# Weight sums of the attention stage on GpSimd, moved tiles of stage two, and one hand-written order for stages 3 to 5

## The chip, the cores and the metric

The kernel runs on one core of a Trainium2 chip. Its engines work side by side, each through its own queue in order: TensorE (PE; its weight loads are shown apart as PEld), VectorE (DVE), ScalarE (ACT), GpSimd (POOL) and SyncE (SP), which here only issues DMAs. GpSimd issues DMAs too, among its other work. An instruction starts when everything ahead of it in its queue has gone and the semaphores that it waits for have been raised. The metric is the device time of one launch in microseconds (us), the median of several runs.

## The reference, cut to what matters

One layer of a streaming encoder over 2048 prompt tokens and 64 sample tokens, width 1024. Three sub-layers follow each other, each with a norm ahead and one behind, whose result is added to the residual:

```python
y = token_mixer(rms_norm(x, g_mixpre), ...)         # gated convolution + matrix memory, one output projection
x = x + rms_norm(y, g_mixpost)
y = memory_attend(rms_norm(x, g_mempre), mk, mv, w_q, w_o)   # 4 heads, 256 memory tokens
x = x + rms_norm(y, g_mempost)
up = causal_dwconv(rms_norm(x, g_ffnpre) @ w_up, ff_buf, w)  # 2 x 2816 columns, width 3
a, g = jnp.split(up, 2, axis=-1)
x = x + rms_norm((gelu(g) * a) @ w_down, g_ffnpost)
```

All matrices are float32. The kernel keeps the precision by splitting an operand into a high part and a remainder and adding three products (high x high, high x remainder, remainder x high).

## The kernel before

The program has five stages, written by `phase1` to `phase5`. Stage 1 projects the input, stage 2 runs the matrix memory and the output projection and leaves x1 in memory, stage 3 is the attention and leaves x2, stage 4 is the up-projection with the convolution, and stage 5 is the down-projection. PE works nearly throughout.

**Splits.** `split` (lines 102 and 103) makes the high part on ScalarE and the remainder on VectorE, or on GpSimd where it is asked for. `mm3` (lines 116 to 118) issues the three products. One split tile is thus written by two engines before PE may read it.

**Stage 2 and the place of A.** The tiles come from pools that are stacked on the left side of SBUF: ld, wp, wk and l2, in that order. When stage 2 ends, stage 3 lays A (64 KB in each partition) and behind it B on the same place. A holds the keys multiplied into the query projection, B the values multiplied into the output projection. A tile of stage 3 waits for the last reader of whatever lay in its place. In wp lie, in this order, the two yn tiles, from which x1 is stored, the gain gb, the residual xt, the second half of the output weights and the states cn.

**Start of stage 3.** PE makes 32 blocks pA of A, six PSUM tiles deep. Each is evicted into A by ScalarE (line 108) and VectorE (line 109). In this part ScalarE, VectorE and GpSimd keep the written order. One tile of raw values, raw4, is loaded three times and is split on GpSimd twice.

**Loop of stage 3.** 16 groups of 128 tokens. A round of PE is: scores (sc, two halves of 24 products), transposition of x of a later group (line 1073, tile tp), a half of the output product (yo), transposition of the finished rows of the group before (line 1229, `x2_T`), then the rest of yo with a transposition of the softmax between. Lines 1073 and 1229 take turns on three PSUM tiles tp, so that the second half of line 1229 needs a tp that VectorE has emptied (the remainder xs, line 103). `x2n` needs a reciprocal root that GpSimd computes by a power (line 96, r2), `post` one more (por), `score` a third (rsr).

**Weight sums.** Beside this, `sums` prepares stage 4, which computes its products by a scheme with seven instead of eight block products and needs sums of weight blocks. 44 pieces of 512 KB are loaded by SP in four DMAs each into a buffer of three, four sums of 128x256 are formed (lines 1141 to 1144), and GpSimd stores the piece. From the fourth round on there are four pieces in a round until they run out. SP also loads the rows xr of x1 for each round, which wait until line 1229 has read the rows before.

**What sets the order.** Within `manual_schedule` the named engines keep the order in which the code is written; the other engines are ordered by a scheduler. PE is in such an order in stages 2 to 5, SP in the loop of stage 3 and in stage 4. In stage 5 SP is ordered by the scheduler, and in its last part ScalarE, VectorE and GpSimd keep the written order.

**Stage 5.** `need` loads and splits a group of 256 tokens of the activations (hr into hh), `load_down` loads and splits the three or four weight tiles of a part (raw into dh and dl).

Of the kernel before, what the change touches and what calls it, by code (L numbers as in the profile page):

```python
# [14 lines left out]
P = 128  # L15
D = 1024
# [16 lines left out]
GROUPS = [(0, 392), (392, 384), (776, 384), (1160, 384)]  # L33
NB = 352
NPASS = T // (2 * NB)
PARTS = [3, 3, 4, 4, 4, 4]
CG = dict(mix=0, mem=8, kv=16, ffn=24, mnw=32, cw=36, fw=48)
CST_W = 48 + 132
# [28 lines left out]
class Prog:  # L67
# [68 lines left out]
    def build(self):  # L136
        tc, nc = self.tc, self.nc
        with ExitStack() as es:
            cp = self.pool(es, "const")

            self.pool(es, "edge", side="right").pool.tile([P, 8], F32, name="edge")
            self.rawp = self.pool(es, "raw", side="right")
            self.ident = cp.tile([P, P], F32, name="ident")
            make_identity(nc, self.ident)
            self.ones = cp.tile([P, P], F32, name="ones")
            nc.vector.memset(self.ones, 1.0)
            sm = cp.tile([P, 16 + 2 * NT], F32, name="small")
            self.mhalf, self.bg = sm[:, 0:8], sm[:, 8:16]
            self.r_all, self.rk_all = sm[:, 16:16 + NT], sm[:, 16 + NT:]
            nc.vector.memset(self.mhalf, -0.5)  # L150
            self.cst = cp.tile([P, CST_W], F32, name="cst")
            self.dma(self.cst, self.a["cst"])
            self.dma(self.bg, self.a["bg"].partition_broadcast(P))
            self.G = cp.tile([P, NT, 8], F32, name="G")
            self.aT = cp.tile([P, NR], F32, name="aT")
            self.em = cp.tile([P, NR], F32, name="em")
            self.wsb = cp.tile([P, NR], F32, name="wsb")
            self.wcb = cp.tile([P, NR], F32, name="wcb")
            dt = tc.dram_tile
            self.yaT = dt([4, P, T], F32, name="yaT")  # L160
            self.x2T = dt([KT, P, T], F32, name="x2Td")
            self.hd = dt([NF, P, T], F32, name="hd")
            self.wsd = dt([NF, P, 4, D // 2], F32, name="wsd")
            self.qT = dt([4, P, T], F32, name="qTd")
            self.kvo = dt([T, KVO], F32, name="kvo")
            self.nmd = dt([NR, P], F32, name="nmd")
            self.wd = dt([NR, P], F32, name="wd")
            self.mkd = dt([KT, P, NM], F32, name="mkd")
            self.mvd = dt([KT, P, NM], F32, name="mvd")
            self.od = dt([P, KT, NS_TOK], F32, name="od")  # L170
            self.ys = dt([NS_TOK, D], F32, name="ysd")
            self.x1 = dt([T, D], F32, name="x1d")
            self.x2 = dt([T, D], F32, name="x2d")
            self.pe = mybir.EngineType.PE
            self.zes = es.enter_context(ExitStack())
            self.qes = es.enter_context(ExitStack())
            self.fl_es = ExitStack()
            self.fl = self.pool(self.fl_es, "fill", space=PSUM)
            self.phase1()
            self.phase2()  # L180
            self.phase3()
            self.phase4()
            self.phase5()


    def phase1(self):
# [541 lines left out]
    def phase2(self):  # L728
        tc, nc, a = self.tc, self.nc, self.a
        V = nc.vector  # L730
        with ExitStack() as es:
# [9 lines left out]
            py_ = self.pool(es, "p2py", bufs=3, space=PSUM)  # L741
            ld.tile([P, 16], F32, name="padl")
            wk.tile([P, 16], F32, name="padw")
            yns = [wp.tile([P, D], F32, name="yn2%d" % i) for i in range(2)]
            gb = wp.tile([P, D], F32, name="gb2")
            xt_ = wp.tile([P, D], F32, name="xt2")
            wo1 = wp.tile([P, 2, 4, D], F32R, name="wo1")
            wo = lambda part, k, sl: (self.wo0(part, k) if k < 4 else wo1[:, part, k - 4])[:, sl]
            cn = {16: wp.tile([P, H, VW], F32, name="cn_s"), 0: wp.tile([P, H, VW], F32, name="cn_p")}

            def load_wo(k):
                raw = self.raw(a["w_out"][k])
# [225 lines left out]
    def phase3(self):  # L978
# [6 lines left out]
        A = lambda part, k, sl: ap[:, part, k, sl]  # L985
        B = lambda part, k, sl: bp[:, part, k, sl]
        with ExitStack() as es:
            es.enter_context(tc.manual_schedule(engines={self.pe}))
            py_ = self.pool(es, "p3py", bufs=3, space=PSUM)
            with ExitStack() as es0:  # L990
                zw = self.wop.tile([P, 7168], F32R, tag="w", name="zw")
                raw4 = self.wop.tile([P, D], F32, tag="w7", name="raw4")
                mv = zw[:, 0:4096].rearrange("p (a k m) -> p a k m", a=2, k=KT)
# [59 lines left out]
            self.em_es.close()  # L1053
            self.wo_es.close()

            es.enter_context(tc.manual_schedule(engines={mybir.EngineType.SP}))
            zq = self.zq = self.pool(self.qes, "zq", side="right")
            zq.tile([P, 32], F32, name="padq")
            wx = self.pool(es, "p3x", side="right")
# [70 lines left out]
            def sums():  # L1130

                KH = KT // 2
                for f in range(NF):
                    for q in range(2):
# [3 lines left out]
                            for h in range(2):  # L1138
                                self.dma(t[:, i + 2 * h], src[:, h].rearrange("p k c -> p (k c)"))
                        a11, a21, a12, a22 = (t[:, i] for i in range(4))  # L1140
                        V.tensor_tensor(out=a22, in0=a21, in1=a22, op=ALU.add)
                        V.tensor_tensor(out=a21, in0=a11, in1=a21, op=ALU.subtract)
                        V.tensor_tensor(out=a11, in0=a22, in1=a11, op=ALU.subtract)
                        V.tensor_tensor(out=a12, in0=a12, in1=a11, op=ALU.subtract)
                        self.store(self.wsd[f, :, :, q * 2 * P:(q + 1) * 2 * P], t)
                        yield

# [87 lines left out]
    def phase4(self):  # L1235
# [12 lines left out]
        self.zes.close()  # L1248
        self.zes = ExitStack()
        with ExitStack() as es:  # L1250
            es.enter_context(tc.manual_schedule(engines={self.pe, mybir.EngineType.SP}))
            left = self.pool(es, "p4l")
            early = self.pool(es, "p4e", side="right")
            right = self.pool(es, "p4r", side="right")
# [45 lines left out]
            def w_split(w, n):  # L1300
                if w is None:
                    return
                if n == "wd":
                    o = left.tile([P, 2, KH, P], F32R, tag="wd", name="wd", bufs=1)
                else:
                    o = first.pop(n, None)
                    if o is None:
                        o = w_op(n, 2 if n == "wc" else 1)
                self.split(o[:, 0], o[:, 1], w.r[n])
                w.o[n] = o  # L1310
# [100 lines left out]

            tk = t_load(0)
            w = w_load(0, ("wb",), tk.w)
            w_split(w, "wa")
            t_split(0, tk, "B11", tk.r["R11"])
            t_split(0, tk, "B21", tk.r["R21"])
            v = head1(0, w, tk.o)
            t_adds(tk)
            t_split(0, tk, "T2", tk.X)
            w_split(w, "wb")  # L1420
            head2(v, tk.o)
            t_split(0, tk, "T1", tk.r["R12"])
# [76 lines left out]
    def phase5(self):  # L1499
        tc, nc, a = self.tc, self.nc, self.a  # L1500
        V = nc.vector
        with ExitStack() as es:
            es.enter_context(tc.manual_schedule(engines={self.pe}))
            ac0 = self.pool(es, "p5a")
            w0 = self.pool(es, "p5w")
            ac1 = self.pool(es, "p5b")
# [36 lines left out]
            def need(i):  # L1543
                if i < len(work) and i not in hs:
                    pi, t0 = work[i]
                    hs[i] = load_h(f0s[pi], PARTS[pi], t0)
            ws = {0: load_down(0, 0, PARTS[0])}
            need(0)
            held = None
            tail = None  # L1550
            for i, (pi, t0) in enumerate(work):
                last = pi == len(PARTS) - 1
                if t0 == groups[3] and pi + 1 < len(PARTS):
                    ws[pi + 1] = load_down(pi + 1, f0s[pi + 1], PARTS[pi + 1])
                if i == len(PARTS):
                    self.dma(gpost, a["g_ffnpost"].partition_broadcast(P))
                if last and tail is None:
# [1 line left out]
                                                                        mybir.EngineType.DVE, mybir.EngineType.Pool})) or 1  # L1559
                need(i)  # L1560
                need(i + 1)
                h = hs.pop(i)
                for j in range(t0 // P, (t0 + min(2 * P, T - t0) + P - 1) // P):
                    w = tw(j)
# [116 lines left out]
```

## Time and profile before

| | us |
|---|---|
| median of 3 runs | 2924.99 |
| lowest and highest | 2923.73, 2928.92 |
| the profiled execution | 2930.46 |
| its span, first to last instruction | 2928.8 |
| PE busy | 2839.5 (97%) |
| DVE, ACT, POOL busy | 1718.0, 1205.7, 383.4 |

Times in the rows further below count from the start of the span. A row of the timeline says when an instruction or a run of equal ones began, how long it took, and in brackets how long the engine had stood idle before it and who released it. By the matmuls' starts stage 2 ends at about 1008 us, the loop of stage 3 lies between 1071 and 1492 us, stage 4 begins with a matmul at 1501 us, and stage 5 with one at 2414 us.

### The profile page before, as it was taken

What the parts mean: (1) busy time and instruction counts of PE and PEld (TensorE: products, weight loads), DVE (VectorE), ACT (ScalarE), POOL (GpSimd) and SP (SyncE); (2) the same over time, 40 slices, a digit from 0 to 9 for tenths busy, and PEclk for the clock granted to TensorE, in tenths of its full rate; (3) what the DMA queues carried; (4) which work ended last, traced back from release to release, by engine and by line L of the source; (5) the groups of instructions that cost most, each with busy time, mean ns of one, the idle gap of its engine ahead of it and who ended that gap; (6) DMA issues with size and microseconds to landing.
All of it is one profiled execution on the core that took longest, in us unless ns stands there. A gap on an engine that the chain in (4) does not pass through costs nothing.

```text
span 2928.8 us, 41744 instructions
## 1 busy us (share of the span) xinstructions
PE 2839.5 (97%) x15906; PEld 2625.9 (90%) x15906; DVE 1718.0 (59%) x2815; ACT 1205.7 (41%) x2463; POOL 383.4 (13%) x608
## 2 busy tenths in 40 slices
PE   8999999999999999999979999999999999999998
PEld 8999999998888877778769999999999988888887
DVE  6413422355666565566567778877887772534459
ACT  5224223233444353332345656566666654101113
POOL 1111011112212111222100000000000000000026
PEclk9999999999999999999989999999999999999999
DMA  8434332147676344677456454654454543322126
GB/s 279 149 100 126 106 114 91 60 150 268 217 223 220 101 145 135 219 235 252 158 183 216 153 174 136 218 173 153 151 181 156 175 132 102 96 62 81 58 79 214
DMA packets 211498, 456.84 MB, mean 156 GB/s; under 512 B 25414, under 2 KB 113672, under 8 KB 211298
## 3 DMA queue, kind: packets, MB, share of 16 engines
q1 hardware_dynamic: 180418, 346.14, 37.6%
q0 software_dynamic: 28720, 100.17, 9.0%
q10 hardware_dynamic: 2160, 7.87, 0.9%
q8 instruction: 125, 2.05, 0.3%
q14 instruction: 75, 0.61, 0.1%
HBM read 345.56 MB, written 108.54 MB: 155 GB/s over the span
## 4 chain that ended last, share of the span: by engine, by line
PE 51%; DVE 6%; DMA 3%; issue 2%; SPq 1%; ACT 1%; POOL 0%; DVEq 0%; POOLq 0%; ACTq 0%
PE up L116 10%; PE up L118 10%; PE up L117 10%; PE y L117 4%; PE y L118 4%; PE y L116 4%; DMA sums<-in_w_up 3%; DVE acc L568 1%; SPq L72 1%; PE yo L116 1%; PE yo L117 1%; PE yo L118 1%; PE sc L116 1%; PE sc L118 1%; PE sc L117 1%
## 5 line engine op out<-in xcount | busy, mean ns | idle before, releaser
L116 PE MATMUL y<-dh,hh 128*128 128x512 f32 x704 | 275.0, 391 | 5.1 <-ACT dh L102 5.1
L117 PE MATMUL y<-dl,hh 128*128 128x512 f32 x704 | 274.8, 390 | 2.4 <-DVE dl L103 2.4
L118 PE MATMUL y<-dh,hh 128*128 128x512 f32 x704 | 274.8, 390 | 0.0
L116 PE MATMUL mm<-xs,wh 128*128 128x384 f32 (+2 forms) x768 | 249.1, 325 | 9.6 <-ACT xs L108 7.3
L118 PE MATMUL mm<-xs,wl 128*128 128x384 f32 (+2 forms) x768 | 248.5, 324 | 1.6 <-DVE wl L103 1.6
L117 PE MATMUL mm<-xs,wh 128*128 128x384 f32 (+2 forms) x768 | 248.8, 324 | 0.0
L1580 DVE TENSOR_TENSOR acc<-y,acc 128x512 f32<-128x512 f32 x170 | 115.5, 689 | 181.3 <-PE y L118 180.5
L116 PE MATMUL up<-B,wa 128*128 128x352 f32 x528 | 172.4, 326 | 8.8 <-ACT wa L102 8.8
L116 PE MATMUL up<-T,wb 128*128 128x352 f32 x528 | 172.1, 326 | 3.8 <-ACT wb L102 3.2
L116 PE MATMUL mmb<-bh,xs 128*128 128x384 f32 (+1 forms) x512 | 173.4, 339 | 0.0
L118 PE MATMUL up<-B,wa 128*128 128x352 f32 x528 | 170.1, 322 | 3.2 <-DVE wa L103 3.2
L118 PE MATMUL mmb<-bh,xs 128*128 128x384 f32 (+1 forms) x512 | 172.5, 337 | 0.0
L117 PE MATMUL mmb<-bl,xs 128*128 128x384 f32 (+1 forms) x512 | 172.4, 337 | 0.0
L117 PE MATMUL up<-T,wb 128*128 128x352 f32 x528 | 170.4, 323 | 1.7 <-DVE T L103 1.7
L117 PE MATMUL up<-B,wa 128*128 128x352 f32 x528 | 170.4, 323 | 0.1
L118 PE MATMUL up<-T,wb 128*128 128x352 f32 x528 | 169.8, 322 | 0.5 <-DVE wb L103 0.5
L116 PEld LDWEIGHTS y<-dh,hh 128*128 128x128 f32 x704 | 132.7, 188 | 33.0 <-ACT dh L102 5.4
L117 PEld LDWEIGHTS y<-dl,hh 128*128 128x128 f32 x704 | 132.6, 188 | 30.4 <-DVE dl L103 3.1
L75 POOL DMA_DIRECT2D hd<-da x88 | 47.4, 541 | 851.4 <-DVE da L1482 823.1
L102 ACT CAST hh<-hr 128x1024 fp32r<-128x1024 f32 (+3 forms) x54 | 49.3, 914 | 263.8 <-PE y L118 262.7
L118 PEld LDWEIGHTS y<-dh,hh 128*128 128x128 f32 x704 | 132.6, 188 | 28.0 <-DVE hh L103 0.5
L116 PEld LDWEIGHTS mm<-xs,wh 128*128 128x128 f32 x768 | 145.5, 190 | 10.6 <-ACT xs L108 7.7
(462 smaller groups left out, 7869.0 us busy)
## 6 DMA issues: line engine op xcount, KB each, us to landing
ws<-wsd SPq DMA_DIRECT2D x132, 512.0 KB, 4.4
raw<-in_w_up SPq DMA_DIRECT2D x66, 512.0 KB, 5.5
raw<-in_wA SPq DMA_DIRECT2D x47, 512.0 KB, 3.6
sums<-in_w_up SPq DMA_DIRECT2D x176, 128.0 KB, 4.3
wsd<-sums POOLq DMA_DIRECT2D x44, 512.0 KB, 4.0
wr<-in_w_up SPq DMA_DIRECT2D x66, 256.0 KB, 4.6
xt<-in_x SPq DMA_DIRECT2D x32, 512.0 KB, 4.4
hr<-hd SPq DMA_DIRECT2D x32, 512.0 KB, 3.9
```

The source lines that it names most:

```text
L72: self.nc.sync.dma_start(out=out, in_=in_)
L75: self.nc.gpsimd.dma_start(out=out, in_=in_)
L102: nc.scalar.copy(hi, src)
L116: nc.tensor.matmul(out, lhsT=lh, rhs=rh, start=(first and i == 0), stop=False, skip_group_check=more)
L117: nc.tensor.matmul(out, lhsT=lh, rhs=rl, start=False, stop=False, skip_group_check=more)
L118: nc.tensor.matmul(out, lhsT=ll, rhs=rh, start=False, stop=(last and i == n - 1), skip_group_check=more)
L568: nc.vector.scalar_tensor_tensor(out=yn[:w, sl], in0=yn[:w, sl], scalar=r[:w, 0:1], in1=xt[:w, sl], op0=ALU.mult, op1=ALU.add)
L1580: V.tensor_tensor(out=acc[j][:, sl], in0=pt, in1=acc[j][:, sl], op=ALU.add)
```

## The change

Three edits. The four sums of a weight piece are formed by GpSimd in place of VectorE. Stage 2's tiles yn2, xt2 and cn come from the pool l2, behind wk, and no longer from wp. The hand-written order for PE and SP now is one scope from the middle of stage 3 to the end, so that stage 5 has SP in the written order too; with it some calls at the start of stages 4 and 5 are written in another order and get a higher priority for the scheduler, and in stage 5 a part's weights are loaded behind the two next groups of activations.

```diff
+HEAD = 120
...
-            self.phase3()
-            self.phase4()
-            self.phase5()
+            with ExitStack() as self.ms:
+                self.phase3()
+                self.phase4()
+                self.phase5()
...
-            yns = [wp.tile([P, D], F32, name="yn2%d" % i) for i in range(2)]
+            yns = [l2.tile([P, D], F32, name="yn2%d" % i) for i in range(2)]
...
-            xt_ = wp.tile([P, D], F32, name="xt2")
+            xt_ = l2.tile([P, D], F32, name="xt2")
...
-            cn = {16: wp.tile([P, H, VW], F32, name="cn_s"), 0: wp.tile([P, H, VW], F32, name="cn_p")}
+            cn = {16: l2.tile([P, H, VW], F32, name="cn_s"), 0: l2.tile([P, H, VW], F32, name="cn_p")}
...
-            es.enter_context(tc.manual_schedule(engines={mybir.EngineType.SP}))
+            self.ms.enter_context(tc.manual_schedule(engines={self.pe, mybir.EngineType.SP}))
...
-                        V.tensor_tensor(out=a22, in0=a21, in1=a22, op=ALU.add)
-                        V.tensor_tensor(out=a21, in0=a11, in1=a21, op=ALU.subtract)
-                        V.tensor_tensor(out=a11, in0=a22, in1=a11, op=ALU.subtract)
-                        V.tensor_tensor(out=a12, in0=a12, in1=a11, op=ALU.subtract)
+                        nc.gpsimd.tensor_tensor(out=a22, in0=a21, in1=a22, op=ALU.add)
+                        nc.gpsimd.tensor_tensor(out=a21, in0=a11, in1=a21, op=ALU.subtract)
+                        nc.gpsimd.tensor_tensor(out=a11, in0=a22, in1=a11, op=ALU.subtract)
+                        nc.gpsimd.tensor_tensor(out=a12, in0=a12, in1=a11, op=ALU.subtract)
...
-            w_split(w, "wa")
-            t_split(0, tk, "B11", tk.r["R11"])
+            with tc.high_priority(offset=HEAD):
+                w_split(w, "wa")
+                t_split(0, tk, "B11", tk.r["R11"])
+                t_adds(tk)
+                t_split(0, tk, "T2", tk.X)
+            v = head1(0, w, tk.o)
             t_split(0, tk, "B21", tk.r["R21"])
-            v = head1(0, w, tk.o)
-            t_adds(tk)
-            t_split(0, tk, "T2", tk.X)
...
-            ws = {0: load_down(0, 0, PARTS[0])}
-            need(0)
+            with tc.high_priority(offset=HEAD):
+                need(0)
+                ws = {0: load_down(0, 0, PARTS[0])}
...
-                if t0 == groups[3] and pi + 1 < len(PARTS):
-                    ws[pi + 1] = load_down(pi + 1, f0s[pi + 1], PARTS[pi + 1])
...
                 need(i)
                 need(i + 1)
+                if t0 == groups[3] and pi + 1 < len(PARTS):
+                    ws[pi + 1] = load_down(pi + 1, f0s[pi + 1], PARTS[pi + 1])
```

On VectorE a steady round of the stage 3 loop reads as follows before; yn, por and r2r belong to the norm behind, sm and sc to the scores, xs to the transposed rows.

```order
L568 SCALAR_TENSOR_TENSOR yn_10174<-yn_10174,por,xr 128x512 x2
L1101 TENSOR_SCALAR sm_11639<-rsr 128x1
L94 TENSOR_SCALAR r2v<-ss_11626 128x1
L1141 TENSOR_TENSOR sums<-sums 128x256
L1108 TENSOR_REDUCE sm_11639<-sc_11641 128x2
L1128 TENSOR_SCALAR xr<-yn_10174,r2r 128x1024
L1109 TENSOR_SCALAR sm_11639<-sm_11639 128x2
L1142 TENSOR_TENSOR sums<-sums 128x256
L1143 TENSOR_TENSOR sums<-sums 128x256
L1144 TENSOR_TENSOR sums<-sums 128x256
L1115 RECIPROCAL sm_11639<-sm_11639 128x2
L1116 TENSOR_TENSOR pp<-pp,sm_11639 128x512
```

The same place of VectorE in the changed kernel, whose line numbers are one or two higher:

```order
L570 SCALAR_TENSOR_TENSOR yn_10175<-yn_10175,por,xr 128x512 x2
L1103 TENSOR_SCALAR sm_11640<-rsr 128x1
L95 TENSOR_SCALAR r2v<-ss_11627 128x1
L1110 TENSOR_REDUCE sm_11640<-sc_11642 128x2
L1111 TENSOR_SCALAR sm_11640<-sm_11640 128x2
L1130 TENSOR_SCALAR xr<-yn_10175,r2r 128x1024
L1117 RECIPROCAL sm_11640<-sm_11640 128x2
L1118 TENSOR_TENSOR pp<-pp,sm_11640 128x512
L1110 TENSOR_REDUCE sm_11640<-sc_11683 128x2
L1111 TENSOR_SCALAR sm_11640<-sm_11640 128x2
L104 TENSOR_TENSOR xs_11716<-tp,xs_11716 128x512 x2
```

The sums are gone from between r2v and the scores, and the second step of the scores (line 1111 now) stands ahead of the product xr.

On GpSimd a steady round before holds the three powers, the stores of the pieces (wsd), of the rows (x2d) and of the transposed rows (x2Td):

```order
L75 DMA wsd<-sums 512x1x256
L75 DMA x2Td<-xg 128x8x128
L75 DMA wsd<-sums 512x1x256 x2
L96 TENSOR_TENSOR por<-pov,small 128x1
L96 TENSOR_TENSOR rsr<-rsv,small 128x1
L75 DMA wsd<-sums 512x1x256
L75 DMA x2d<-yn_10174 128x1024
L96 TENSOR_TENSOR r2r<-r2v,small 128x1
```

The stretch of GpSimd in the changed kernel from the third piece of a round on (two pieces of four sums and a store each stand ahead of it):

```order
L1143 TENSOR_TENSOR sums<-sums 128x256
L76 DMA wsd<-sums 512x1x256
L1144 TENSOR_TENSOR sums<-sums 128x256
L97 TENSOR_TENSOR por<-pov,small 128x1
L97 TENSOR_TENSOR rsr<-rsv,small 128x1
L1145 TENSOR_TENSOR sums<-sums 128x256
L1146 TENSOR_TENSOR sums<-sums 128x256
L76 DMA wsd<-sums 512x1x256
L76 DMA x2d<-yn_10175 128x1024
L97 TENSOR_TENSOR r2r<-r2v,small 128x1
```

por and rsr now stand behind ten sums and two stores of the same round, and r2r behind two more sums and a third store.

On SP the passage from stage 4 to stage 5 before, where raw<-in_w_down are stage 5's weights and hr its activations:

```order
L72 DMA raw<-in_w_down 128x1024
L72 DMA ws<-wsd 128x1024
L72 DMA raw<-in_w_down 128x1024
L72 DMA ws<-wsd 128x1024
L72 DMA wr_22451<-in_w_up 128x512
L72 DMA raw<-in_w_down 128x1024
L72 DMA hr<-hd 128x3x256 x2
```

The same passage now:

```order
L73 DMA ws<-wsd 128x1024 x2
L73 DMA wr_22448<-in_w_up 128x512
L73 DMA hr<-hd 128x3x256
L73 DMA raw<-in_w_down 128x1024 x3
L73 DMA hr<-hd 128x3x256 x3
```

The three weight tiles have moved from between the last loads of stage 4 to behind the first load of activations. PE's order is the same throughout, and so are those of ScalarE and VectorE at the passages from stage 2 to 3 and from 3 to 4.

## Rows read from the trace of the kernel before

**Rows 1.** Who PE waited for, whole span: us in total, times, longest.
```profile
PE tp L1229 <- DVE xs L103: 18.2, 8, 4.2
...
PE pA L116 <- DVE A L109: 6.5, 4, 4.1
```

**Rows 2.** Stretches: us, busy of PE, PEld, DVE, ACT, POOL; granted clock, DMA share, GB/s.
```profile
1264.40:1267.70 3.30, 3.30 (x11) 2.72 (x10) 2.25 (x5) 0.24 (x2) 0.02 (x1) 0.51 0.48 137
1015.20:1021.90 6.70, 4.41 (x19) 4.11 (x20) 4.63 (x9) 5.03 (x10) 1.97 (x1) 0.50 0.26 84
```

**Rows 3.** VectorE's timeline: start, us, instruction, run length, idle before and releaser.
```profile
1244.29 0.42 DVE L1141 TENSOR_TENSOR sums<-sums 128x256 f32<-128x256 f32 x1 [0.87 <-DMA sums<-in_w_up]
...
1258.49 0.42 DVE L1141 TENSOR_TENSOR sums<-sums 128x256 f32<-128x256 f32 x1 [3.84 <-DMA sums<-in_w_up]
...
1259.43 0.75 DVE L1128 TENSOR_SCALAR xr<-yn,r2r 128x1024 f32<-128x1024 f32 x1
...
1263.31 1.28 DVE L103 TENSOR_TENSOR xs<-tp,xs 128x512 fp32r<-128x512 f32 x2
```

**Rows 4.** PE's timeline in the loop of stage 3.
```profile
1237.35 0.66 PE L1229 MATMUL tp<-ident,xr 128*128 128x128 f32 x4 [1.14 <-DVE xs L103]
...
1264.05 1.00 PE L1229 MATMUL tp<-ident,xr 128*128 128x128 f32 x4 [1.98 <-DVE xs L103]
...
1275.24 0.39 PE L116 MATMUL sc<-A,xs 128*128 128x512 f32 x1
...
1299.68 0.39 PE L116 MATMUL sc<-A,xs 128*128 128x512 f32 x1
```

**Rows 5.** GpSimd's timeline in the same round.
```profile
1251.16 0.67 POOL L96 TENSOR_TENSOR por<-pov,small 128x1 f32<-128x1 f32 x1 [0.93 <-DVE rsv L94]
1251.81 0.54 POOL L96 TENSOR_TENSOR rsr<-rsv,small 128x1 f32<-128x1 f32 x1
1252.31 0.71 POOL L75 DMA_DIRECT2D wsd<-sums  x1
1253.58 0.56 POOL L75 DMA_DIRECT2D x2d<-yn  x1 [0.56 <-DVE sm L1101]
1254.80 0.56 POOL L96 TENSOR_TENSOR r2r<-r2v,small 128x1 f32<-128x1 f32 x1 [0.66 <-DVE r2v L94]
```

**Rows 6.** Groups on GpSimd, whole span: busy us, mean ns, idle before.
```profile
L562 POOL TENSOR_TENSOR acc<-acc,gpost 128x512 f32<-128x512 f32 x30 | 48.3, 1629 | 14.1 <-ACT junk L558 14.1
L103 POOL TENSOR_TENSOR zw<-raw,zw 128x1024 fp32r<-128x1024 f32 x3 | 7.2, 2411 | 5.6 <-ACT zw L102 5.6
L562 POOL TENSOR_TENSOR fo<-fo,gpost 64x512 f32<-64x512 f32 x2 | 2.5, 1286 | 418.5 <-ACT junk L558 418.5
```

**Rows 7.** Groups on VectorE, stage 3's loop.
```profile
L568 DVE SCALAR_TENSOR_TENSOR yn<-yn,por,xr 128x512 f32<-128x512 f32 x32 | 22.6, 748 | 8.2 <-POOL por L96 8.2
L1141 DVE TENSOR_TENSOR sums<-sums 128x256 f32<-128x256 f32 x44 | 18.6, 423 | 64.6 <-DMA sums<-in_w_up 64.6
```

**Rows 8.** Groups on VectorE, last 98 us of the span.
```profile
L568 DVE SCALAR_TENSOR_TENSOR acc<-acc,por,xt 128x512 f32<-128x512 f32 x32 | 37.1, 1200 | 0.7 <-POOL por L96 0.7
```

**Rows 9.** Passage from stage 2 to 3, PE's timeline, then VectorE's.
```profile
1017.07 0.58 PE L116 MATMUL pA<-mk,hi 128*128 128x256 f32 x1 [4.05 <-DVE A L109]
...
1009.47 0.69 DVE L562 TENSOR_TENSOR yn<-yo,gb 128x512 f32<-128x512 f32 x1 [2.03 <-ACT yn L558]
```

**Rows 10.** The same passage, ScalarE's timeline, then GpSimd's.
```profile
1016.03 0.47 ACT L108 ACTIVATE A<-pA,cst 128x256 fp32r<-128x256 f32 x1 [6.59 <-issue]
...
1012.88 0.57 POOL L75 DMA_DIRECT2D x1d<-yn  x1 [1.75 <-DVE yn L568]
```

**Rows 11.** Passage from stage 4 to 5, SP's timeline, then ScalarE's.
```profile
2404.44 0.96 SPq L72 DMA_DIRECT2D hr<-hd  x2
...
2413.05 2.94 ACT L102 CAST dh<-raw 128x1024 fp32r<-128x1024 f32 x3
```

**Rows 12.** DMA issues, 2395 to 2425 us: count, KB each, median us to landing.
```profile
raw<-in_w_down SPq DMA_DIRECT2D x4, 512.0 KB, 5.1
```

More of the change, by code (lines that the diff above doesn't have):

```diff
@@ L987, in phase3 @@
         with ExitStack() as es:
-            es.enter_context(tc.manual_schedule(engines={self.pe}))
             py_ = self.pool(es, "p3py", bufs=3, space=PSUM)
             with ExitStack() as es0:
+                es0.enter_context(tc.manual_schedule(engines={self.pe}))
                 zw = self.wop.tile([P, 7168], F32R, tag="w", name="zw")
@@ L1250, in phase4 @@
         with ExitStack() as es:
-            es.enter_context(tc.manual_schedule(engines={self.pe, mybir.EngineType.SP}))
             left = self.pool(es, "p4l")
@@ L1502, in phase5 @@
         with ExitStack() as es:
-            es.enter_context(tc.manual_schedule(engines={self.pe}))
             ac0 = self.pool(es, "p5a")
```

## The prediction

> **What bounds the kernel now.** The table of engines comes first: PE is busy 2839.5 of 2928.8 us, so the time can only fall where PE stands still or runs at half clock, and an engine that is moved work to matters only where PE comes to wait for it. Next the table of waits [rows 1]: the largest item is the second half of the transposition of x2 (line 1229), which waits eight times for VectorE's remainder xs, 18.2 us in all; another is A at the head of stage 3 with 6.5. Then the stretches behind those waits [rows 2]: in the second row PE is busy 4.41 us at a granted clock of 0.50, which is 1.2 instead of 2.4 GHz, so a wait is paid twice, once standing and once in half of the time worked after it (first row: 3.30 us at 0.51, 1.6 lost; there are four such stretches in the loop, behind four of the eight waits, 6.5 us together). Both places are touched by the change. Last the timelines, to see why VectorE and ScalarE are late there [rows 3 to 5, 9, 10].
>
> In the loop VectorE takes the sums in its written order, and a sum stands before everything behind it until its piece has landed. The sum at 1258.49 starts after 3.84 us of idling for a DMA, the norm's product xr follows at 1259.43, xs at 1263.31 [rows 3], and PE gets its tp 1.98 us late [rows 4]. Over the loop the first sums of the 44 pieces have 64.6 us of such idle ahead of them [rows 7]. So the loop holds 18.2 + 6.5 = 24.7 us that could be had.
>
> **Moved tiles of stage 2.** Before, ScalarE's first write of A begins at 1016.03 after 6.59 us of idling; the store of x1 from yn, which had to leave A's place, was issued at 1012.88 for 0.57 [rows 10], and PE, six PSUM tiles deep, stands 4.05 us at 1017.07 [rows 9]. With yn, xt and cn out of wp, the last reader in A's place is VectorE's product with gb, 1009.47 + 0.69 = 1010.2 [rows 9]: the first write can begin 5.9 us earlier, ahead of PE's seventh block. This removes 4.1 + 0.4 us of waiting and half of 4.41 us at half clock, 2.2, so 6.7. One microsecond I take back: the GpSimd splits that follow for the second use of raw4 stay as long as they are (2.41 us per 128x1024 [rows 6] and their loads), and an earlier PE meets them earlier. Result **-5.7**; bounds -6.9 (all, and B earlier too) and -3 (raw4's splits take half of it). The same stores now meet B's place, which is written far behind their landing: 0.
>
> **Sums on GpSimd.** VectorE loses 4 x 44 x 0.42 = 74 us, and the blocking for pieces with them. But por, rsr, x2d's issue and r2r stand behind the sums of three pieces on GpSimd now, and the new wait is VectorE's product L570 for por: behind it in its queue are sm, r2v, the steps of the scores, the product xr and xs, for which PE waits. So the loop from one transposition to the next has to be closed, and compared with a round that did not wait: scores at 1275.24 to 1299.68, 24.44 us [rows 4]. The steps are: SP loads the rows and then the pieces once PE has read the rows (1237.35 + 0.66 = 1238.01), and the first of three pieces lies there at 1244.29, 6.3 us [rows 3, 4]; 12 sums of s each; three stores of 0.71, por 0.67, rsr 0.54, x2d 0.56, r2r 0.56, 4.5 us [rows 5], plus 0.1 to reach VectorE; from xr's product to the first xs done 1259.43 to 1263.95, less three sums and one step of the scores that no longer lie between, 3.0 [rows 3]; the transpositions 0.6. That is 14.5 + 12 s, and PE waits from s = 0.83 us on.
>
> The trace has no 128x256 product on GpSimd. Bounds by the nearest rows [rows 6]: a quarter of the 128x1024, 2411 ns, gives 0.60; the line through 128x512 (1629) and 128x1024, drawn down to 256 elements, 1.24. The line through 64x512 (1286) and 128x1024 gives 2.2 ns an element and 0.16 fixed, 0.73 for 256. I take 0.73 and 0.04 between two sums that follow each other, 0.77, since the 1629 row lies between VectorE's work in the norms and has probably been held up. Then the loop is 23.7. But products of VectorE beside those of GpSimd are stretched: L568 takes 748 ns in the loop and 1200 in the last 98 us, where GpSimd multiplies beside it [rows 7, 8]; one such pair lies in a round, 0.7 us. That makes 24.4 against 24.44: no slack. I charge 0.5 us in each of about 9.5 rounds with four pieces, 5 us, 1 us for the round at 1155 where the pieces begin, and give back 4 of the 6.5 us of clock, as some small waits will stay: 18.2 - 6 + 4 = **-16**. Own bounds: -24.7 (s = 0.60, no wait) and, for s = 1.24, a loss (below).
>
> The Trainium skill (GPSIMD Engine Reference, Elementwise — side-by-side cycle accounting) gives a product of two tensors about 2.6 cycles an element at 1.2 GHz on GpSimd, an estimate of 0.55 us for 256 elements plus dispatch, and keeps elementwise work on VectorE as a rule; the 2411 ns for 1024 elements in rows 6 agree with the cycles. By it the loop would be some 22 us and the whole 24.7 us would come back. On the stretched products its page SBUF — State Buffer (Who interferes with whom) says that a VectorE instruction with two SBUF inputs and a GpSimd instruction that reads SBUF exclude each other; the 748 and 1200 ns agree.
>
> **The one order and the later weights.** PE's order is the same throughout, ScalarE's and VectorE's until stage 5, and the passage from stage 3 to 4 as a whole: 0. On SP three weight tiles went behind the first load of activations. That load is issued at 2404.44 and ScalarE makes the first high part of a weight at 2413.05 [rows 11], 8.6 us later, while a load of 512 KB lands 5.1 us after its issue [rows 12]. With one load of activations ahead of three of weights the last weights are there between 2408 and 2413. Below nothing: the activations, now first, can at most be there earlier, but ScalarE is still on stage 4's last work, so no gain. Taken 0, bounds 0 and +8.
>
> **Sum.** -5.7 - 16 + 0 = -22, from the profiled execution's 2930.5 to 2908.5; the median of the runs lies 5.5 lower than the profiled one, so 2903, and I say **2902**.
>
> **Rivals.**
> - GpSimd too slow by a little, s between 0.92 and 1.05: the loop takes 25.5 to 27.1, 1.1 to 2.7 us over in 9.5 rounds, 10 to 25 lost of the 30.4 (24.7 + 5.7) that are there: 2905 to 2920, the middle 2912. For it speaks the 1629 ns row, against it the 64x512 one.
> - GpSimd much too slow, the slower side: with s = 1.24 the loop takes 29.4, 5 us over in 9.5 rounds, +47, against those 30.4, +17, and a clock that falls after each wait: 2942, up to 2957 with 1.6 us in each round. It decides from 12 s x 9.5 over 30.4, s = 1.1. Only the line through the two 128-row groups speaks for it.
> - The weights of stage 5 come late: the loads issued together land one behind the other and behind the activations, up to 8 us later than now, and PE waits 3 to 8 us more: 2905 to 2910.
> - The change doesn't free A: something else in the place keeps the first write at 1016, and only the loop's 16 come: 2909.
>
> **How the numbers follow.** The main case has 58%, between 2893 (the loop's whole 24.7 with 6.9 at A) and 2912; a little too slow 17%, much too slow 12%, late weights 8%, A not freed 5%. The range goes from 2891 to 2924, which leaves out the much slower case and a little below. A measurement of this kernel can't tell less than 0.2%, 5.9 us, from no change. Faster takes the main case, the weights, A and most of the little-too-slow, less a tenth for what I haven't seen: 0.78; same 0.10; slower 0.12, the second rival.
>
> **What would show it.** Right: the wait of line 1231's tp for xs gone or under 6 us; the first write of A near 1010 us and no stretch at half clock behind it; sums on GpSimd of at most 0.83 us, its busy time up by some 140 us and VectorE's down by about 74; the rounds 24.4 to 25. Wrong: por seen 3 us or more late in every round, with L570 waiting for it and PE for xs; sums of 1 us and over; in stage 5 dh waiting for a DMA after 2413 less what was won before.

## The result: 1.3% slower

The changed kernel takes 2963.2 us (median of 4 runs, 2959.1 to 2965.1) against 2924.4 before (4 runs); the ratio is 1.0128 [1.011, 1.0145]. Forecast were 2902, between 2891 and 2924, and faster with 0.78: wrong in sign. The profiled execution has a span of 2963.3 us against 2928.8.

Cut at the first matmul of each part, the two spans differ as follows (us).

| part | before | changed | difference | forecast |
|---|---|---|---|---|
| stages 1 and 2 | 1008.6 | 1011.1 | +2.5 | 0 |
| building A and B | 62.1 | 56.3 | -5.8 | -5.7 |
| loop of stage 3, to the first matmul of stage 4 | 430.5 | 437.9 | +7.4 | -16 |
| stage 4 | 912.9 | 913.0 | +0.1 | 0 |
| stage 5 to its last matmul, and what follows | 514.6 | 545.0 | +30.4 | 0 |

The difference in the first row can't be told from chance: in the fourteen kernels below, whose stages 1 and 2 are those of the changed kernel, it lies between 1005.0 and 1010.0, on both sides of the 1008.6. Two others carry the loss, the loop and stage 5.

The table of waits of the changed kernel (us in total, times, longest), against [rows 1]:

```profile
PE tp L1231 <- DVE xs L104: 24.9, 11, 5.2
PE y L117 <- ACT hh L103: 15.4, 6, 4.2
...
PE pA L117 <- DVE A L110: 2.6, 3, 1.4
```

The wait for xs, which was to go, has grown from 18.2 in eight to 24.9 in eleven. A wait for hh is there that before had no row of a microsecond. Of the three only A's wait fell, from 6.5 to 2.6. At A, ScalarE's first write now follows PE (ScalarE's timeline, to compare with [rows 10], where the trace names no releaser; that it was the store of x1 is the prediction's reading):

```profile
1012.77 0.48 ACT L109 ACTIVATE A<-pA,cst 128x256 fp32r<-128x256 f32 x1 [0.81 <-PE pA L119]
```

It idles 0.81 us, not 6.59.

**The loop after.** GpSimd's timeline over one round of the changed kernel, then VectorE's and PE's, which answer to [rows 3 to 5]:

```profile
1267.97 0.74 POOL L1143 TENSOR_TENSOR sums<-sums 128x256 f32<-128x256 f32 x1 [2.60 <-DMA sums<-in_w_up]
1268.78 0.74 POOL L1144 TENSOR_TENSOR sums<-sums 128x256 f32<-128x256 f32 x1
...
1276.74 0.81 POOL L1144 TENSOR_TENSOR sums<-sums 128x256 f32<-128x256 f32 x1
1277.43 0.63 POOL L97 TENSOR_TENSOR por<-pov,small 128x1 f32<-128x1 f32 x1
...
1279.35 1.07 POOL L1146 TENSOR_TENSOR sums<-sums 128x256 f32<-128x256 f32 x1
1280.72 0.73 POOL L76 DMA_DIRECT2D wsd<-sums  x1 [0.30 <-POOL sums L1146]
...
1282.44 0.56 POOL L97 TENSOR_TENSOR r2r<-r2v,small 128x1 f32<-128x1 f32 x1 [0.44 <-DVE r2v L95]
```

```profile
1273.03 0.15 DVE L95 TENSOR_SCALAR pov<-poss 128x1 f32<-128x1 f32 x1
...
1278.10 2.88 DVE L570 SCALAR_TENSOR_TENSOR yn<-yn,por,xr 128x512 f32<-128x512 f32 x2 [4.84 <-POOL por L97]
...
1283.65 0.74 DVE L1130 TENSOR_SCALAR xr<-yn,r2r 128x1024 f32<-128x1024 f32 x1
...
1285.26 1.07 DVE L1118 TENSOR_TENSOR pp<-pp,sm 128x512 f32<-128x512 f32 x1
...
1287.10 1.28 DVE L104 TENSOR_TENSOR xs<-tp,xs 128x512 fp32r<-128x512 f32 x2
```

```profile
1260.83 0.65 PE L1231 MATMUL tp<-ident,xr 128*128 128x128 f32 x4 [2.35 <-DVE xs L104]
...
1287.84 0.66 PE L1231 MATMUL tp<-ident,xr 128*128 128x128 f32 x4 [2.31 <-DVE xs L104]
```

pov is ready at 1273.2, and por begins 4.2 us later, behind the sums; VectorE stands 4.84 us for it with everything behind, and PE gets its tp 2.31 us late. From one such transposition to the next are 27.0 us, where PE needs 24.4. The granted clock did not fall behind every such wait. Of the ten longest waits for xs in this loop it fell behind three (at 1152.53, 1368.77 and 1424.32). Two stretches of 4 us behind a wait, the first at a granted clock of 1.00, the second at 0.60 (columns as in [rows 2]):

```profile
1260.83:1264.83 4.00, 4.00 (x23) 3.46 (x24) 2.60 (x5) 1.15 (x5) 0.47 (x2) 1.00 0.84 244
1368.77:1372.77 4.00, 4.00 (x13) 3.39 (x14) 2.59 (x5) 0.59 (x3) 1.02 (x2) 0.60 0.73 249
```

**Stage 5 after.** SyncE's timeline in the last part, then ScalarE's and VectorE's and PE's:

```profile
2865.89 2.04 SPq L73 DMA_DIRECT2D out_y<-acc  x2
2868.02 0.39 SPq L73 DMA_DIRECT2D hr<-hd  x1
2868.50 0.51 SPq L73 DMA_DIRECT2D xt<-x2d  x1
2877.13 2.03 SPq L73 DMA_DIRECT2D out_y<-acc  x2
...
2882.03 2.03 SPq L73 DMA_DIRECT2D out_y<-acc  x2
2884.15 0.39 SPq L73 DMA_DIRECT2D hr<-hd  x1
```

```profile
2872.95 1.04 ACT L103 CAST hh<-hr 128x1024 fp32r<-128x1024 f32 x1 [6.76 <-DMA hr<-hd]
...
2889.33 1.04 ACT L103 CAST hh<-hr 128x1024 fp32r<-128x1024 f32 x1 [7.01 <-DMA hr<-hd]
```

```profile
2874.02 1.22 DVE L104 TENSOR_TENSOR hh<-hr,hh 128x1024 fp32r<-128x1024 f32 x1 [5.10 <-ACT hh L103]
...
2881.26 2.44 DVE L570 SCALAR_TENSOR_TENSOR acc<-acc,por,xt 128x512 f32<-128x512 f32 x2
```

```profile
2874.04 0.79 PE L117 MATMUL y<-dh,hh 128*128 128x512 f32 x1 [4.15 <-ACT hh L103]
```

The activations hr of the next group stand on SP behind the stores out_y of an earlier one, which VectorE's L570 releases. Issued at 2868.02, they reach ScalarE's cast at 2872.95, VectorE at 2874.02; its sums and norms follow, the L570 at 2881.26 releases the next stores, and these the next hr at 2884.15. It is a closed circle of 16.4 us (2872.95 to 2889.33). Before, a load lay a group further ahead, on the other side of such stores: counted from the end, the load at 2849.72 belongs to the cast at 2867.68, 18 us later, where it is 4.9 now (SyncE's timeline, then ScalarE's):

```profile
2849.72 0.38 SPq L72 DMA_DIRECT2D hr<-hd  x1
2851.57 2.05 SPq L72 DMA_DIRECT2D out_y<-acc  x2
...
2860.71 0.38 SPq L72 DMA_DIRECT2D hr<-hd  x1
```

```profile
2856.69 1.03 ACT L102 CAST hh<-hr 128x1024 fp32r<-128x1024 f32 x1
2867.68 1.03 ACT L102 CAST hh<-hr 128x1024 fp32r<-128x1024 f32 x1
```

There a group took 11.0 us. In the last part the six intervals between one cast of hh and the next are 15.6 to 16.7 us now and were 10.1 to 11.0 before. From the first cast to the last it is 96.9 us against 65.0, which is the whole of the 30.4.

### The profile page after: what moved, and what is told of

The parts are those of the page before. It is cut to its first block, busy times and chain, and to the rows that moved or that the text cites. A ratio compares the mean times of both kernels' runs of the same rounds, so it can differ in the third digit from the quotient of the medians.

```text
span 2963.3 us, 41688 instructions
## 1 busy us (share of the span) xinstructions
PE 2853.0 (96%) x15906; PEld 2632.6 (89%) x15906; DVE 1680.7 (57%) x2639; ACT 1206.4 (41%) x2463; POOL 516.5 (17%) x784
## 4 chain that ended last, share of the span: by engine, by line
PE 49%; DVE 6%; DMA 3%; POOL 3%; issue 2%; ACT 2%; SPq 1%; POOLq 0%; DVEq 0%; ACTq 0%
PE up L117 10%; PE up L119 10%; PE up L118 10%; PE y L118 4%; PE y L119 4%; PE y L117 4%; DMA sums<-in_w_up 2%; DVE acc L570 1%; DVE yn L570 1%; DMA hr<-hd 1%; SPq L73 1%; POOL sums L1144 1%; PE yo L117 1%; PE yo L118 1%; DVE acc L1582 1%
## 5 line engine op out<-in xcount | busy, mean ns | idle before, releaser
L117 PE MATMUL y<-dh,hh 128*128 128x512 f32 x704 | 279.6, 397 | 20.5 <-ACT hh L103 15.4
L119 PE MATMUL y<-dh,hh 128*128 128x512 f32 x704 | 278.9, 396 | 2.6 <-DVE hh L104 2.5
```

Source lines behind the costliest of these rows:

```text
L117: nc.tensor.matmul(out, lhsT=lh, rhs=rh, start=(first and i == 0), stop=False, skip_group_check=more)
L119: nc.tensor.matmul(out, lhsT=ll, rhs=rh, start=False, stop=(last and i == n - 1), skip_group_check=more)
```

## The experiments

Times are medians beside the kernel before on the same chip (2926 to 2930 in these runs). The three parts are cut as above, each from one profiled execution. How far such a part varies by itself is seen where the loop was not altered: 434.9 to 438.5 in the changed kernel, e2 and e3, and 429.0 to 430.5 in the kernel before, e1 and e4.

| run | time | ratio [95%] | A, B | loop | stage 5 to last matmul |
|---|---|---|---|---|---|
| e1 sums back on VectorE | 2949.1 | 1.0074 [1.0058, 1.0089] | 56.2 | 429.1 | 533.6 |
| e2 SP by scheduler in stage 5 | 2930.1 | 1.0006 [0.9997, 1.0014] | 56.2 | 438.5 | 504.2 |
| e3 hr a group earlier | 2929.8 | 1.0012 [1.0002, 1.0023] | 56.3 | 434.9 | 503.8 |
| e4 only the moved tiles | 2922.6 | 0.9987 [0.9977, 0.9996] | 56.3 | 429.0 | 504.7 |
| e5 rows late | 2955.7 | 1.0093 [1.0078, 1.0109] | 56.3 | 434.9 | 531.3 |
| e6 two sums of four | 2950.9 | 1.0073 [1.0059, 1.0088] | 56.3 | 430.6 | 533.5 |
| e7 before, tiles, rows late | 2912.6 | 0.9943 [0.993, 0.9957] | 56.3 | 418.0 | 504.7 |
| e8 e2 with rows late | 2926.1 | 0.9993 [0.9983, 1.0004] | 56.3 | 436.0 | 504.2 |
| e9 e2 without powers | 2896.1 | 0.9899 [0.9885, 0.9914] | 56.3 | 402.3 | 504.8 |
| e10 e7, sums a piece later | 2912.5 | 0.9959 [0.9943, 0.9974] | 56.2 | 415.3 | 504.0 |
| e11 e4, sums a piece later | 2913.3 | 0.9954 [0.9938, 0.9969] | 56.5 | 426.5 | 504.2 |
| e12 e2, rows by ScalarE | 2999.4 | 1.0256 [1.0239, 1.0273] | 56.3 | 504.6 | 504.0 |
| e13 e2, powers first | 2902.9 | 0.9909 [0.9892, 0.9925] | 56.2 | 410.8 | 503.9 |
| e14 e13, last rows | 2897.3 | 0.9886 [0.9869, 0.9903] | 56.3 | 404.1 | 503.9 |

**e1, the sums back on VectorE.** The four lines of the sums read `V.` for `nc.gpsimd.` again.

> The changed kernel with the four sums of a piece back on VectorE, all else as changed. Theory: the stage 3 loop is what the sums cost; by the two traces it went from 429.0 us (1072.2 to 1501.2) to 436.4 (1069.0 to 1505.3), so 7.4 us come back: about 2956 against 2963.2, the waits of the second half of the x2 transposition back to some 18 us in eight, the tail of stage 5 as slow as in the changed kernel. Rival one (the sums are innocent, the one scope for the order slows the loop): 2963, loop still 436. Rival two (GpSimd's sums also slow the end of stage 5): 2930 or less.

The loop is at 429.1, as before; stage 5 stays slow. The sums are the loop's loss, and not stage 5's. The time is 2949.1 where 2956 was expected; in the profiled execution stages 1 and 2 are 4.4 us shorter than in the changed kernel's, which is no effect of the sums, as they come later.

**e2, SP by the scheduler in stage 5.**

```diff
             with ExitStack() as self.ms:
                 self.phase3()
                 self.phase4()
-                self.phase5()
+            self.phase5()
...
+            es.enter_context(tc.manual_schedule(engines={self.pe}))
```

> The changed kernel with SP ordered by the scheduler again in stage 5 (PE stays in the written order), all else as changed, the calls of stage 5 in their new order and with their priority. Theory: the written order of SP puts the load of a group's activations behind the stores of the group before last; that costs the last part 16.4 us a group in place of 11.0, some 30 us; they come back: 2933 (2963.2 - 30), and PE's waits for hh in the last part go from 15.4 us to under 1. Rival (the weights that are loaded behind the activations, or the priorities, make it slow): 2955 or more.

504.2: the 30 us are back, with the calls in their new order and with their priority. The rival falls.

**e3, only the load earlier, SP in the written order.** `fetch` issues a group's load alone, and the split follows where it was.

```diff
...
                 need(i + 1)
+                if last:
+                    fetch(i + 2)
```

> The changed kernel; in the last part of stage 5 alone the load of a group's activations (not its split) is written one group earlier, so that on SP it stands ahead of the stores that it stood behind. SP keeps the written order. Theory (the load's place in SP's order closes a circle through VectorE: stores, load, split, sums, stores): a group takes 11 us again, 27 to 30 us come back, 2934 to 2937. Rival one (the splits and the norm on VectorE and GpSimd got longer by themselves): still 2963. Rival two (the loss is at the start of stage 5 or in its weights): still 2963, with the loss elsewhere.

503.8, and the casts of hh come every 11.0 us again. So not SP's order as such, but the place of this one load in it is the whole loss of stage 5.

**e4, only the moved tiles.**

> The kernel before with yn2, xt2 and cn moved to the other pool and nothing else. Theory: what the two traces show at A, 3.2 us (stage 3's loop begins at 1069.0 in place of 1072.2): 2921 against 2924.4. The prediction had 5.7: 2918.7. Rival (the 3.2 us come from the other edits, or are given back at the next wait): 2924.

The stretch of A and B is 56.3 against 62.1. The expectation's 3.2 was read from clock times shifted by the 2.5 us of the first stages; the forecast's 5.7 holds in this stretch. The ratio's interval, 1.2 to 6.7 us, takes in both figures, so the total time does not decide between them.

**e5 and e8, the rows' load behind two pieces** (e8 with e2's edit besides).

```diff
                 yos = []
-                if s.c < 15:
-                    xr = zq.tile([P, D], F32, tag="xr", name="xr", bufs=1)
-                    self.dma(xr, self.x1[s.c * P:(s.c + 1) * P])
...
                             yield
+                            if s.c < 15 and nh == 0:
+                                xr = zq.tile([P, D], F32, tag="xr", name="xr", bufs=1)
+                                self.dma(xr, self.x1[s.c * P:(s.c + 1) * P])
```

> The changed kernel; in the stage 3 loop the load of the rows xr is written behind the loads of two pieces in place of ahead of them, so that on SP these pieces no longer stand behind a load that waits for the transposition of x2. Theory: the loop is a closed circle (transposition, rows and pieces, twelve sums, the powers behind them, product, remainder xs, transposition) of 27.0 us; with two pieces loaded beforehand it falls below the 24.4 us that PE needs, the stretch from the loop's start to stage 4 goes from 437.9 to 410 to 420, the time to about 2940 (stage 5 stays slow, 533 us). Rival (GpSimd or the port that it shares with VectorE is too slow for the sums wherever they stand): stretch 435 to 440, time 2960.

> The changed kernel with both repairs: SP by the scheduler in stage 5, and the load of the rows behind the loads of two pieces. Theory: stage 5 at 504 us, the loop at 410 to 420, A at 56: 2902 to 2912. If this is faster than the kernel with the sums on VectorE and the same place of the rows' load, the sums are better off on GpSimd; if slower, they were worse there in any order. Rival (GpSimd too slow for the sums): 2930 as with stage 5's repair alone.

434.9 and 436.0: a miss, and no difference from an unaltered loop that could be told. Between two loads of rows SP still has four pieces, and the scheduler put por behind nine sums in a row, as it had behind ten: other pieces, a circle much like it. That the rival's stretch was measured doesn't prove the rival: e9 and e13 decide. What was expected of e8 also says that a time above that with the sums on VectorE would make GpSimd the worse place in any order. e8 is slower than e7, but e14 is faster, so this does not follow.

**e6, two of the four sums left out.**

> The changed kernel with two of the four sums of a piece left out, so the stored sums are not the reference's. Theory: the twelve sums that lie on the circle become six; at 0.81 us from one to the next the round is 27.0 - 4.9 = 22.1, below PE's 24.4, the waits for xs go and the loop stretch falls from 437.9 to about 412, the time to about 2937. Rival (the loads of the pieces set the round, not the sums): stretch over 430. The step between says what a sum costs on the path.

430.6 in place of 412: a miss too, 7 us in place of 26. The scheduler gave GpSimd another order with it, as its timeline shows:

```profile
1322.54 0.64 POOL L97 TENSOR_TENSOR por<-pov,small 128x1 f32<-128x1 f32 x1
1323.09 0.61 POOL L97 TENSOR_TENSOR rsr<-rsv,small 128x1 f32<-128x1 f32 x1
1327.97 0.98 POOL L1143 TENSOR_TENSOR sums<-sums 128x256 f32<-128x256 f32 x1 [4.28 <-DMA sums<-in_w_up]
...
1330.98 0.65 POOL L97 TENSOR_TENSOR r2r<-r2v,small 128x1 f32<-128x1 f32 x1
```

r2r now stands behind a sum whose piece has not landed, and GpSimd idles 4.28 us for it. It is what VectorE did before [rows 3], moved to another engine. So this run doesn't give the price of a sum: fewer of them helped, but what the powers stand behind changed too.

**e9, the powers off GpSimd.** In the loop the three powers are replaced by a product on VectorE.

> The changed kernel with SP by the scheduler in stage 5, and in the stage 3 loop the powers (por, rsr, r2r) left out: VectorE writes a product of the same 128x1 tiles in their place, so the norms there are not the reference's. The sums stay on GpSimd in their order. Theory: the loop is slow because these three small results stand behind sums in GpSimd's queue; with them gone nothing on PE's way waits for GpSimd, the loop stretch goes from 438.5 to 405 to 415, the time to about 2905. Rival one (the loads of the pieces set the round): stretch 430 or more. Rival two (VectorE's instructions are lengthened by GpSimd's sums beside them): 425 or more.

402.3, with 2.2 us of gaps in the loop ahead of stage 4 and one wait of PE for xs (PE's table of waits, 1060 to 1480 us):

```profile
PE tp L1237 <- DVE xs L108: 0.3, 1, 0.3
```

All 176 sums are still on GpSimd beside VectorE (means of 799 to 852 ns), and VectorE's product with por is still lengthened by them (mean 1085 ns; 1184 in the changed kernel, 748 before). Neither the loads of the pieces nor this lengthening sets the round.

**e12, the rows by ScalarE's queue.**

```diff
-                    self.dma(xr, self.x1[s.c * P:(s.c + 1) * P])
+                    nc.scalar.dma_start(out=xr, in_=self.x1[s.c * P:(s.c + 1) * P])
```

> The changed kernel with SP by the scheduler in stage 5 and with the rows xr loaded by ScalarE's queue, so that SP never stands for the transposition of x2; sums on GpSimd. Theory (the round is a circle that goes through SP's wait): pieces land ahead of their turn, GpSimd has at most one piece before it when a power comes up, the stretch goes from 438.5 to 408 to 418, time about 2907. Rival (GpSimd's order, not the loads: the powers stand behind as many sums as before): stretch 430 or more, time 2925 or more.

504.6, the other way altogether. SP now loads pieces whenever a buffer is free, and between r2r at 1242.0 and the next por at 1276.4 GpSimd stores seven pieces, where the changed kernel has three between 1255.4 and 1277.4. VectorE's waits in the loop, of e12 and then of the changed kernel:

```profile
DVE yn L570 <- POOL por L97: 107.9, 15, 18.9
```

```profile
DVE yn L570 <- POOL por L97: 53.7, 16, 6.4
```

**e13, the same powers first.** GpSimd keeps a written order in the loop: por, the rows' store, r2r, rsr, then three pieces; the load of the rows stands one piece ahead of the next por. Shown without the lines that take this load out of its old place.

```diff
...
+            es.enter_context(tc.manual_schedule(engines={mybir.EngineType.Pool}))
             ch = {0: xT(0)}
...
                 if i != 1:
                     next(ws, None)
+                if i > 2:
+                    next(ws, None)
                 next(g, None)
...
                 if i > 2:
                     next(ws, None)
+                if i < 15:
+                    ch[i].xr = zq.tile([P, D], F32, tag="xr", name="xr", bufs=1)
+                    self.dma(ch[i].xr, self.x1[i * P:(i + 1) * P])
                 next(ws, None)
...
-                if i > 1:
-                    next(ws, None)
                 next(y)
```

> The changed kernel with SP by the scheduler in stage 5; the powers stay on GpSimd, and GpSimd keeps a written order in the stage 3 loop: por, the store of the rows, r2r, rsr, then the sums of three pieces that were loaded ahead of the rows, then those of the one piece that is loaded behind them. Theory (the powers' place behind sums is the whole loss): as without the powers, stretch 402 to 412, time 2896 to 2906. Rival one (it was GpSimd's share of VectorE's reads, which went when VectorE wrote the results itself): stretch 425 or more. Rival two (sixteen sums, four stores and the loads don't fit between two powers): 430 or more, with por waiting for the last piece.

410.8, and 404.1 with e14's one load moved. GpSimd's timeline of e14, where r2r now follows por in 3.5 us with no sum between:

```profile
1278.56 0.73 POOL L76 DMA_DIRECT2D wsd<-sums  x1 [0.30 <-POOL sums L1146]
1279.24 0.63 POOL L97 TENSOR_TENSOR por<-pov,small 128x1 f32<-128x1 f32 x1
1281.62 0.59 POOL L76 DMA_DIRECT2D x2d<-yn  x1 [1.75 <-DVE rsv L95]
1282.79 0.56 POOL L97 TENSOR_TENSOR r2r<-r2v,small 128x1 f32<-128x1 f32 x1 [0.57 <-DVE r2v L95]
1283.33 0.85 POOL L97 TENSOR_TENSOR rsr<-rsv,small 128x1 f32<-128x1 f32 x1
1283.84 0.89 POOL L1143 TENSOR_TENSOR sums<-sums 128x256 f32<-128x256 f32 x1
```

The powers are on the same engine beside the same sums. Two things differ from e2, the powers' place and that of the rows' load: por stands behind one piece that is loaded after the rows and no longer behind ten sums, r2r behind none. The rows' load in another place had brought nothing that could be told by itself (e5, e8), and with the powers off GpSimd the loads as they were had been no hindrance (e9): the powers' place behind the sums was the loop's loss. In e13 PE stood 15.7 us ahead of stage 4, because the last rows' load, on GpSimd's queue, had come behind a store.

**e14, the last rows by ScalarE's queue.**

```diff
-                                self.store(xr, self.x1[s.c * P:(s.c + 1) * P])
+                                nc.scalar.dma_start(out=xr, in_=self.x1[s.c * P:(s.c + 1) * P])
```

> The kernel of the last run (powers ahead of the sums on GpSimd) with one load moved: the rows of the last group go out by ScalarE's queue in place of GpSimd's. Theory: the 15.7 us that PE stands at the start of stage 4 there, 7 more than in the kernel before, come from GpSimd's written order, in which this load stands behind the store of the transposed rows (issued at 1462.7, the norm's product waits for it until 1470.7); with it gone 5 to 7 us come back, the loop stretch goes from 410.8 to about 404, the time to about 2896. Rival (the last norm is late for another reason, or ScalarE's queue issues it no earlier): 410, 2903.

The wait is 9.1 and the time 2897.3, 0.9886 [0.9869, 0.9903] of before: the fastest that computes everything.

**e7, e10 and e11, the sums on VectorE, with more lead.** e7 is e4 with the late rows; in e10 and e11 the next piece's load is written ahead of a piece's sums.

> The kernel before with the moved tiles of stage two and with the load of the rows xr behind the loads of two pieces; sums on VectorE, SP by the scheduler in stage 5. Theory: VectorE's waits for pieces come from loads that stand behind the rows on SP; with them gone the loop loses most of its 21 us of gaps and some 6 us of half clock: stretch 429 to about 410, time 2900 to 2908. Rival (the pieces come late because there are three buffers and each is stored before it is loaded again): stretch 425 to 430, time as with the moved tiles alone, 2922.

> The kernel before with the moved tiles, the rows' load behind two pieces, and the sums of a piece written one piece later, behind the loads of the next; sums on VectorE. Theory: what is left of the loop's waits with the late rows alone (12.5 us of gaps in 418.0) are sums that stand in VectorE's order before their piece has landed; a piece more of lead takes most of them: stretch about 408, time about 2903. Rival (three buffers: the next load waits for the store of an earlier piece, which now comes later): stretch 418 or more.

> As the last, but with the rows' load where it was, ahead of two pieces. Theory (lead is what counts, wherever it is won): stretch between 410 and 420 in place of 429.0, time about 2910. Rival (only the rows' place counts): 429, 2922.

418.0, 415.3 and 426.5: the late rows take 11 us of the loop, somewhat over half of what was expected. What the lead adds, 2.5 to 2.7 us, is no more than an unaltered loop varies by, so e10 and e11 are misses. With the sums on VectorE moving the load does help; why it helps there and not in e5 and e8 was not tested. A difference between e7 and e10 in total time is not told from these runs.

## Why the prediction was wrong

Of the 61 us between 2902 and 2963, 30.4 are stage 5 and 23.4 the loop (+7.4 in place of -16).

**A: right, and to a tenth by luck.** 5.8 us against 5.7, and 5.6 to 5.9 in each kernel with the moved tiles, by the step that the prediction gave: the first write no longer waits, and the granted clock between 1011 and 1067 us is 1.00, 0.95 in this part before. But of the wait of 4.05 us 0.55 stays, the clock gave 1.9 us and not 2.2, and the microsecond taken back for raw4's splits was not lost; these three cancel.

**The loop: the mechanism right, the sum wrong.** The step "14.5 + 12 s" closed the circle as it is, and the wait for por with xs behind it is the one that was named. It came out 24.4 against PE's 24.44 and measured 27.0, as follows.

| piece of the circle | forecast | measured |
|---|---|---|
| rows read to first piece there | 6.3 | 6.5 |
| twelve sums, stores, powers | 12 x 0.77 + 4.5 = 13.7 | 15.0 |
| to xr's product | 0.1 | 0.65 |
| to the first xs done | 3.0 | 4.1 |
| transposition | 0.6 | 0.65 |
| beside each other's reads | 0.7 | in the above |

s itself was well sized: 0.73 to 0.74 alone, 0.81 from one start to the next (0.77 forecast). But with no slack each small term was a loss in every round: 0.30 us from a last sum to its store, a sum of 1.07 beside VectorE's product with por, 0.44 for r2v, 0.65 for xr's product behind a step of the scores, 0.7 for the exponentials and 1.07 for the product pp in place of 0.69. The 0.7 that were charged for this should have been 3.3. Part of it is the path: r2r's last 0.44 us are no queue of GpSimd's but a wait for r2v, which comes by way of L570 and ScalarE.

In the sum 18.2 - 6 + 4 both terms failed. The waits for xs, which were to fall from 18.2 to 6, rose to 24.9: charged were 0.5 us a round, and PE stood some 2.3 us. Of the half clock 4 us were to come back and none did: PE's busy time in the loop is 401.2 us, 400.3 before and 392.4 in e9. Together that is the +7.4, but for 0.2. The rival "GpSimd too slow by a little" had the mechanism with s at 0.92 to 1.05 and ended at 2905 to 2920, as it counted the half clock as won; with A and the loop alone (e2) it is 2930, which is also outside the range.

The Trainium skill's page SBUF — State Buffer, section Who interferes with whom, has it that a VectorE instruction with two SBUF inputs and a GpSimd instruction that reads SBUF exclude each other. The trace agrees: the two L570 of a round took 1.41 us before and 2.88 beside the sums (1278.10), 1.47 more where 0.7 were charged for the pair.

**Stage 5: the step that failed.** "The one order and the later weights" looked at SP's order only where stage 4 ends, and priced 0 with +8 at most for weights that come late. The weights cost nothing (PE's wait for dh is 5.1 us as before). But the same scope gives SP the written order to the end, and in the last part the written place of hr lies behind stores: 16.4 us a group in place of 11.0, 30.4 in all, and none of it with that one load moved (e3). No rival had it, and the range had no room for 30 us. The passage was taken for the whole of stage 5, while SP's order had changed to its last row.

## What to carry to other kernels

When one scope gives a queue the written order, go through that queue to its last row, and for each load ask which store or wait now stands ahead of it and whether what releases that needs the load: a circle through a DMA costs its latency in every round (here 4.9 us from hr's issue to its cast). When bulk work moves to a quieter engine, its busy share (here 51% of the loop) says little; list the small operations that other engines wait for, and put them ahead of the bulk. A loop that is closed by a sum of many terms, and comes out at exactly the time that is there, is to be forecast as a loss.

## What the runs showed of the hardware

Instructions of one or two elements are lengthened too when they meet a GpSimd sum: the 128x1 addition poss took 1.00 us at 1271.99 in the changed kernel against 0.15 at 1250.41 before, and the 128x2 step of the scores 0.75 (1282.98) against 0.22 (1260.09). The first cost nothing in this round, as por began only at 1277.43. The second did: xr's product started behind it at 1283.65, though r2r was there at 1283.00.
